# Expert capacities in unequal pairs, the sort of places behind the routing, and the last norm ahead of the overflow test

## The chip, the cores and the metric

The kernel runs on one core of a Trainium2 chip. The metric is the device time of one execution in microseconds (us). TensorE (PE) multiplies and loads its weights (PEld), VectorE (DVE), ScalarE (ACT) and GpSimd (POOL) do the rest, and SyncE (SP) issues nearly all of the large transfers. All data is fp32.

## The reference, cut to what matters

Two transformer blocks follow each other on 256 tokens of width 1024. The second one ends in a mixture of experts, and the change lies there:

```python
def moe_ffn(h, ...):                       # h: 256 tokens x 1024
    logits = h @ w_router + b_router       # 32 experts
    top_val, top_idx = lax.top_k(logits, 4)
    gate_w = softmax(top_val)
    # each token goes to its 4 experts e:
    hb = x[e] @ w_exp_in[e] + b_exp_in[e]  # 1024 -> 2 x 1024
    g, u = min(hb[:1024], 7), clip(hb[1024:], -7, 7)
    a = g * sigmoid(1.702 * g) * (u + 1)
    y = a @ w_exp_out[e] + b_exp_out[e]    # 1024 -> 1024
    # out: sum over the 4 experts of gate_w * y
h = layer_norm(DEEPNORM_ALPHA * h + moe_ffn(h), ln2_g, ln2_b)
```

The weights of one expert are 12 MB in fp32, those of all 32 are 403 MB, and every expert has tokens.

## The kernel before, in words

The first third (37 weight loads of 2 MB, the attention and retention block, the first feed-forward part, the second attention) is untouched. Then comes the router: `chosen` (line 859) takes the top 4 of each token tile, two matmuls with a triangular matrix (lines 913 and 915) number the tokens of each expert, and `pg` (line 917) holds each token's place in its expert.

**Places and capacities.** The 32 experts are worked on in an order of places 0 to 31. Place r has room for `caps(r)` tokens (line 125): 128, 64 or 32. Places 0 and 1 are always experts 0 and 1 (`FIXED`). The other places are given out at run time by `sort_experts` (line 947): the experts are ranked by their number of tokens, and the fullest one gets the place with most room (`_places`, line 1350). The table `SLOTS` (line 27) gives one capacity for each pair of places, so that both places of a pair have the same one; in order: 64, 32, 32, 128, 32, 32, 128, 32, 32, six times 64, 32. If an expert has more tokens than its place holds, `overflow` (line 1199) does the rest; a register load and an `If` on `most` decide that (lines 1151 and 1152).

**One expert.** `gather` (line 1019) runs once for a pair of places, during the odd place before it: it builds one-hot matrices (`one_hots`) and multiplies them with the normed tokens `hn`, 16 matmuls with as many columns as the pair has places for tokens. `hidden` (line 1051) runs 8 matmuls per quarter f of the first layer; since a place with 32 (64) tokens fills only a quarter (half) of the array's columns, 4 (2) of the eight run side by side. `gated` brings the result back into columns (transposes, or the `fold` matmuls where c is 32) and applies the activation, `out_rows` multiplies with the second layer, `weigh` applies the gate on ACT and DVE, and `scatter` (8 matmuls) adds the result to the four accumulators `acc`.

**Weights.** `Stream` (line 43) loads the weights through SP in program order, 2 MB for each transfer (line 69), six for an expert: four for the first layer, two for the second. In the expert stage the ring has nine such slots (three `w`, three `wh`, and `ring2`, `ring3`, `more4`), so a load waits until PE has read what lay in its slot nine loads before. From place 2 on, SP has to know the expert's number: 30 register loads of `ids` (line 152, `part`), placed in SP's queue among the weight loads. `ids` is made in the middle of `sort_experts` (line 977).

**When the sort runs.** `sort_experts` is a generator whose pieces run at the steps named in `SORT` (line 31): the first one, up to the sorted `posm` and `gtok`, is started at place 0 after its third quarter. Its tiles are the accumulators (`scr`), its table `places` is loaded by GpSimd at that point (line 959).

**Second norm.** `normed` (line 849) scales and shifts `hn`. For the first token tile it runs on DVE; for the second one, columns 0 to 511 go to ACT (line 853) and GpSimd (line 854), the others to DVE.

**The end.** After the last `scatter` comes the test for overflow, and after the `If` the last layer norm (lines 1156 to 1196), which writes the output in four transfers.

Within TensorE's queue and the others the order is set by a scheduler at build time, from the program order and estimated durations.

Of the kernel before, what the change touches and what calls it, by code (L numbers as in the profile page):

```python
# [26 lines left out]
SLOTS = (64, 32, 32, 128, 32, 32, 128, 32, 32, 64, 64, 64, 64, 64, 64, 32)  # L27
# [3 lines left out]
SORT = ((0, 2), (0, 3), (3, 1), (18, 1), (20, 1))  # L31
# [93 lines left out]
def caps(r):  # L125

    return SLOTS[r // 2]


def build(nc, tc, ctx, a, dbg=None):  # L130
# [662 lines left out]
    aid = mo.tile([128, 128], F32, name="aid")  # L793
    V.tensor_scalar(aid, ident, ALPHA, None, op0=OP.mult)
# [73 lines left out]
    def one_hots(r0, pos):  # L868

        c = caps(r0)  # L870
        oh = mo.tile([128, 2, 2, 128 // c, c], F32, name="oneh")
        for t in range(2):
            for i in range(2):
                last = V.tensor_scalar(oh[:, t, i], iota[:, None, 1:c + 1].to_broadcast([128, 128 // c, c]),
                                       pos[:, t, r0 + i:r0 + i + 1], None, op0=OP.is_equal)
        return oh, last
# [3 lines left out]
    for t in range(2):  # L880
# [25 lines left out]
        if t == 0:  # L906
            normed(t)
# [39 lines left out]
    def sort_experts():  # L947

        sp = mo
        b = scr[0][:, 0:2 * E].rearrange("p (i e) -> p i e", i=2)  # L950
# [7 lines left out]
        places = ep.tile([128, 128], F32, name="places", bufs=1)  # L958
        nc.gpsimd.dma_start(places, a["places"])
        bw = ep.tile([128, 512], F32, name="xs", bufs=3)  # L960
# [6 lines left out]
        b = scr[1][:, 0:2]  # L967
# [6 lines left out]
        b = scr[2][0:E, 0:2 * E].rearrange("p (i e) -> p i e", i=2)  # L974
# [6 lines left out]
        b = scr[3][:, 0:128]  # L981
# [3 lines left out]
        b = scr[0][:, 0:4 * E].rearrange("p (j t e) -> p j t e", j=2, t=2)  # L985
# [11 lines left out]
        yield  # L997

        bw = ep.tile([128, D], F32, name="xs", bufs=3)
        for t in range(2):  # L1000
            nc.gpsimd.dma_start(bw[64 + t * E:64 + (t + 1) * E, :], a["bout"])
        for n in range(2):
# [16 lines left out]
    def gather(r0):  # L1019
# [3 lines left out]
        c = caps(r0)  # L1023
        oh, _ = first if r0 == 0 else one_hots(r0, posm)
        xs = [ep.tile([128, 8, c], F32, name="xs", bufs=3) for _ in range(2)]
        for i in range(2):
            slots_of[r0 + i] = [xs[i]]
        per = min(8, 256 // c)
        for at, k0 in enumerate(range(0, 8, per)):
            b = (em.tile([128, 512], F32, name="m") if r0 else scr[at])[:, 0:per * 2 * c]  # L1030
            b = b.rearrange("p (k i c) -> p k i c", k=per, i=2)
            for kk in range(per):
# [3 lines left out]
            for i in range(2):  # L1036
                (A.copy if i else V.tensor_copy)(xs[i][:, k0:k0 + per], b[:, :, i, :])
            yield
        for i in range(2):
            b = em.tile([128, 2], F32, name="m")  # L1040
            for t in range(2):
                T.matmul(b, oh[:, t, i].rearrange("p d c -> p (d c)"), gtok[:, t, r0 + i, :],
                         start=t == 0, stop=t == 1)
# [105 lines left out]


# [4 lines left out]

    e1 = pool(ctx, "e1", 1)
    rows = ws.next()
# [269 lines left out]
```

## Time and profile before

| what | value |
|---|---|
| time, median of 3 runs | 1485.1 us (1479.3 to 1487.65) |
| time of the profiled execution | 1477.87 us |
| its span, first to last instruction | 1476.1 us |
| granted TensorE clock, mean | 0.978 of full speed |
| PE busy | 1394.0 us (94%) |
| DVE, ACT, POOL busy | 657.4, 433.6, 36.7 us |
| moved by DMA | 495.15 MB, 335 GB/s over the span |

The page divides the span into 40 slices of 36.9 us. A digit is the busy share in tenths, and the last line the rate of all transfers. The expert stage is in slices 14 to 39. PE reads as busy nearly throughout, also where a matmul only waits in its pipeline, so its busy share says little; the rate of the transfers says more.

### The profile page before, as it was taken

What the parts mean: (1) busy time and instruction counts of PE and PEld (TensorE: products, weight loads), DVE (VectorE), ACT (ScalarE), POOL (GpSimd) and SP (SyncE); (2) the same over time, 40 slices, a digit from 0 to 9 for tenths busy, and PEclk for the clock granted to TensorE, in tenths of its full rate; (3) what the DMA queues carried; (4) which work ended last, traced back from release to release, by engine and by line L of the source; (5) the groups of instructions that cost most, each with busy time, mean ns of one, the idle gap of its engine ahead of it and who ended that gap; (6) DMA issues with size and microseconds to landing.
All of it is one profiled execution on the core that took longest, in us unless ns stands there. A gap on an engine that the chain in (4) does not pass through costs nothing. (4 is left out here: it accounts for less than half of the span.)

```text
span 1476.1 us, 21068 instructions
## 1 busy us (share of the span) xinstructions
PE 1394.0 (94%) x8401; PEld 882.1 (60%) x8402; DVE 657.4 (45%) x1622; ACT 433.6 (29%) x819; POOL 36.7 (2%) x54
## 2 busy tenths in 40 slices
PE   7998999989999899999999899998999999999984
PEld 7988999979999744544545444454343443443431
DVE  5868977866667533222123221232332333233313
ACT  4535655544565212121112211122111111111111
POOL 1001000010001100000000000000000000000000
PEclk9999999999999999899999999999999999999987
DMA  8435545535435989999989999899999999999995
GB/s 350 172 129 184 215 172 199 203 137 200 179 142 197 392 328 365 427 427 426 427 349 418 426 427 426 349 417 427 426 426 428 426 427 426 427 426 427 426 427 213
DMA packets 38008, 495.15 MB, mean 335 GB/s; under 512 B 4561, under 2 KB 4881, under 8 KB 8593
## 3 DMA queue, kind: packets, MB, share of 16 engines
q1 hardware_dynamic: 35424, 486.69, 79.8%
q0 software_dynamic: 2192, 6.88, 1.4%
q8 instruction: 68, 1.11, 0.3%
q14 instruction: 36, 0.29, 0.1%
q10 hardware_dynamic: 288, 0.18, 0.0%
HBM read 492.68 MB, written 1.05 MB: 334 GB/s over the span
## 5 line engine op out<-in xcount | busy, mean ns | idle before, releaser
L1060 PE MATMUL m<-w,xs 128*64 128x512 f32 (+2 forms) x1392 | 315.2, 611 | 10.3 <-DMA w<-in_wexp_dram 10.3
L1077 DVE TENSOR_TENSOR gu<-m,bexp 128x256 f32<-128x256 f32 (+2 forms) x128 | 51.1, 399 | 457.2 <-PE m L1074 310.9
L1060 PEld LDWEIGHTS m<-w,xs 128*64 128x64 f32 (+2 forms) x1392 | 102.3, 136 | 167.9 <-issue 157.3
L1063 ACT COPY hs<-m 128x512 f32<-128x512 f32 x128 | 74.9, 585 | 416.0 <-PE m L1060 416.0
L232 PE MATMUL b<-ah,wh 128*128 128x256 f32 x1552 | 194.3, 282 | 1.4 <-ACT wh L83 1.4
L232 PEld LDWEIGHTS b<-ah,wh 128*128 128x128 f32 x1552 | 187.6, 191 | 3.3 <-ACT wh L83 1.8
L105 DVE TENSOR_TENSOR wh<-w,wh 128x1024 fp32r<-128x1024 f32 (+1 forms) x152 | 174.2, 1180 | 31.7 <-ACT wh L104 31.7
L104 ACT ACTIVATE wh<-w 128x1024 fp32r<-128x1024 f32 (+1 forms) x154 | 148.7, 1019 | 79.8 <-PE b L232 43.4
L1097 PE MATMUL m<-w,ea 128*32 128x512 f32 (+2 forms) x672 | 141.6, 614 | 9.3 <-DMA w<-in_wexp_dram 6.3
L1060 PE MATMUL m<-wh,xs 128*32 128x512 f32 (+2 forms) x656 | 121.4, 597 | 8.4 <-DMA wh<-in_wexp_dram 8.1
L205 DVE SCALAR_TENSOR_TENSOR one<-m,gs,one 128x512 fp32r<-128x512 f32 x64 | 46.8, 749 | 129.1 <-ACT one L204 127.7
L1084 ACT ACTIVATE th<-gu 128x128 f32<-128x128 f32 (+2 forms) x128 | 38.4, 300 | 215.3 <-DVE gu L1082 215.3
L232 PE MATMUL b<-al,wh 128*128 128x256 f32 x776 | 99.4, 280 | 0.0
L232 PEld LDWEIGHTS b<-al,wh 128*128 128x128 f32 x776 | 94.5, 190 | 0.0
L1097 PE MATMUL m<-wh,ea 128*64 128x512 f32 (+2 forms) x352 | 85.5, 627 | 4.9 <-DMA wh<-in_wexp_dram 4.1
L1097 PEld LDWEIGHTS m<-w,ea 128*32 128x32 f32 (+2 forms) x672 | 40.6, 129 | 78.4 <-issue 55.9
L1112 PE MATMUL acc<-one,so 128*128 128x512 f32 x256 | 77.5, 423 | 9.7 <-ACT one L204 8.6
L1072 PEld LDWEIGHTS m<-fold,hs 128*128 128x128 f32 x448 | 56.6, 196 | 48.0 <-issue 35.9
L1060 PEld LDWEIGHTS m<-wh,xs 128*32 128x32 f32 (+2 forms) x656 | 35.5, 124 | 72.4 <-issue 66.0
L1112 PEld LDWEIGHTS acc<-one,so 128*128 128x128 f32 x256 | 43.0, 188 | 50.0 <-ACT one L204 29.0
L1035 PE MATMUL m<-oneh,hn 128*128 128x64 f32 (+2 forms) x480 | 69.0, 299 | 0.0
L204 ACT ACTIVATE one<-m,gs 128x512 fp32r<-128x512 f32 x64 | 42.5, 686 | 82.1 <-PE m L1097 82.0
(370 smaller groups left out, 1384.5 us busy)
## 6 DMA issues: line engine op xcount, KB each, us to landing
w<-in_wexp_dram SPq DMA_DIRECT2D x128, 2048.0 KB, 37.4
wh<-in_wexp_dram SPq DMA_DIRECT2D x63, 2048.0 KB, 37.5
w<-in_wpre_dram SPq DMA_DIRECT2D x37, 2048.0 KB, 7.9
w<-in_wpre_dram SPq DMA_DIRECT2D x4, 512.0 KB, 7.9
w<-in_wexp_dram SPq DMA_DIRECT2D x4, 512.0 KB, 30.3
tab<-in_tab_dram SPq DMA_DIRECT2D x1, 1152.0 KB, 10.0
xn<-in_x_dram SPq DMA_DIRECT2D x2, 512.0 KB, 5.0
ra<-in_rowv_dram POOLq DMA_DIRECT2D x2, 512.0 KB, 7.2
```

Source lines behind the costliest of these rows:

```text
L104: self.nc.scalar.activation(h[:, c], t[:, c], AF.Copy)
L105: self.nc.vector.tensor_tensor(l[:, c], t[:, c], h[:, c].bitcast(F32), op=OP.subtract)
L204: return (A.activation(hi, src, AF.Copy, scale=scale), V.scalar_tensor_tensor(lo, src, scale, hi.bitcast(F32), op0=OP.mult, op1=OP.subtract))
L205: V.scalar_tensor_tensor(lo, src, scale, hi.bitcast(F32), op0=OP.mult, op1=OP.subtract))
L232: T.matmul(p[:, m, :], x[:, k, c], y[:, k, :], start=i == m == k == 0, stop=i == 2 and k == nk - 1, skip_group_check=True)
L1035: T.matmul(b[:, kk], hn[:, t, f], oh[:, t, :, 0, :], start=t == 0, stop=t == 1)
L1060: T.matmul(b[g * c:(g + 1) * c], xs[:, k, :], w[:, kk, :], start=k < n, stop=k >= 8 - n, skip_group_check=True)
L1063: A.copy(h, b)
L1072: T.matmul(p[:, j, :], h[:, j * 128:(j + 1) * 128], fold, start=True, stop=True)
L1077: V.tensor_tensor(both, p[:, :, 0:c], bexp[:, r, f].rearrange("p j i -> p (j i)")[:, :, None].to_broadcast([128, 4, c]), op=OP.add)
L1097: T.matmul(ys[n][g * c:(g + 1) * c], ac[:, kk, :], w[:, kk, n * 512:(n + 1) * 512], start=(j == kk == 0) if c == 128 else j < 64 // c, sto ...
L1112: T.matmul(acc[t][n], so[:, t * 128:(t + 1) * 128], y[:, n, :], start=first and y is yh, stop=last and y is yl, skip_group_check=True)
```

## The change

1. `SLOTS` now has one capacity for each place, and a pair may have two different ones. The three capacities occur as often as before (4 times 128, 14 times 64, 14 times 32); the places with 128 are now 6, 10, 14 and 18, each followed by one with 32, where they were 6, 7, 12 and 13.
2. `gather` writes one tile `xs` for both places of a pair, in two buffers by turns, and copies each group of matmuls with one instruction, on DVE and ACT by turns. The one-hot matrices of a pair lie side by side, and the 16 matmuls take as many columns as both places have together (96, 128 or 160; before 64, 128 or 256).
3. `sort_experts` is cut into more pieces, uses tiles of the pool `em` and not the accumulators, and its first three pieces run between the steps of the first `gather`, before place 0. `places` is loaded long before, into the tile of `aid`, and `aid` is made after the sort.
4. `normed` of the second token tile runs on DVE alone, one half before `pg` and one after the one-hot matrices of places 0 and 1.
5. The last layer norm and the output stand ahead of the register load and the `If`; a second copy of them stands inside the `If`, behind `overflow`.

```diff
-SLOTS = (64, 32, 32, 128, 32, 32, 128, 32, 32, 64, 64, 64, 64, 64, 64, 32)
+SLOTS = ((64, 64, 32, 64, 32, 64) + 3 * (128, 32, 64, 32) + (128, 32, 64, 64) + 5 * (64, 32))
-SORT = ((0, 2), (0, 3), (3, 1), (18, 1), (20, 1))
+SORT = ((0, 1), (0, 2), (2, 1), (2, 3), (18, 1), (20, 1))
 def caps(r):
-    return SLOTS[r // 2]
+    return SLOTS[r]
...
-    def normed(t, *ins):
-        for c in half:
-            if t and not c.start:
-                A.activation(hn[:, t, c], hn[:, t, c], AF.Copy, scale=lr[t])
-                G.tensor_tensor(hn[:, t, c], hn[:, t, c], ln[:, 1, c], op=OP.add)
-                continue
-            with after(*ins):
-                V.scalar_tensor_tensor(hn[:, t, c], hn[:, t, c], lr[t], ln[:, 1, c], op0=OP.mult, op1=OP.add)
+    def normed(t, c, *ins):
+        with after(*ins):
+            V.scalar_tensor_tensor(hn[:, t, c], hn[:, t, c], lr[t], ln[:, 1, c], op0=OP.mult, op1=OP.add)
...
-    normed(1, last)
+    normed(1, half[0], last)
     V.scalar_tensor_tensor(pg[:, 0], b, 1.0, sel, op0=OP.add, op1=OP.mult)
     first = one_hots(0, pg[:, 0])
     done = first[1]
+    normed(1, half[1], done)
...
-        places = ep.tile([128, 128], F32, name="places", bufs=1)
-        nc.gpsimd.dma_start(places, a["places"])
...
-        xs = [ep.tile([128, 8, c], F32, name="xs", bufs=3) for _ in range(2)]
-        per = min(8, 256 // c)
+        xs = ep.tile([128, 8, c], F32, name=f"xs{r0 // 2 % 2}", bufs=1)
+        per = min(8, 512 // c)
...
-                    T.matmul(b[:, kk], hn[:, t, f], oh[:, t, :, 0, :], start=t == 0, stop=t == 1)
-            for i in range(2):
-                (A.copy if i else V.tensor_copy)(xs[i][:, k0:k0 + per], b[:, :, i, :])
+                    T.matmul(b[:, kk], hn[:, t, f], oh[:, t].rearrange("p i c -> p (i c)")[:, 128 - c0:128 + c1],
+                             start=t == 0, stop=t == 1)
+            (A.copy if at % 2 else V.tensor_copy)(xs[:, k0:k0 + n], b)
...
     todo = gather(0)
-    for _ in range(4):
-        next(todo, None)
     pend = None
     sort = sort_experts()
+    for _ in range(3):
+        next(sort)
+        next(todo, None)
...
     scatter(*pend, False, True)
     close(ex2)
+    rows = ws.next()
+    def last_norm(ctx):
...
+    with ExitStack() as so:
+        last_norm(so)
     n = nc.values_load(most[0:1, 0:1], min_val=0, max_val=S)
     with tc.If(n > 0):
         with ExitStack() as so:
             overflow(so, nc, tc, em, a, acc, hn, iota, ident, posm, gtok, bexp, ids, over)
-    e1 = pool(ctx, "e1", 1)
...
+        with ExitStack() as so:
+            last_norm(so)
```

In TensorE's queue, right behind the routing's two matmuls with `sel`, this stands before (`oneh,hn` is the gather, `gtok` the gate columns, `w,xs` the first layer of place 0, and `sel`, `ones`, `pg` belong to the sort):

```order
L913 MATMUL b<-sel,upper 128x64
L915 MATMUL b<-sel,ones 128x32
L1035 MATMUL acc_5287<-oneh,hn 128x128
L1035 MATMUL acc_5288<-oneh,hn 128x128
L1035 MATMUL acc_5287<-oneh,hn 128x128 x7
L1035 MATMUL acc_5288<-oneh,hn 128x128 x7
L1042 MATMUL m<-gtok,oneh 128x2 x4
L1060 MATMUL m<-w_4910,xs 64x512 x4
L1060 MATMUL m<-w,xs 64x512 x4
L953 MATMUL acc_5287<-ones,sel 32x32 x2
```

and this now:

```order
L910 MATMUL b<-sel,upper 128x64
L912 MATMUL b<-sel,ones 128x32
L951 MATMUL m<-ones,sel 32x32 x2
L951 MATMUL m<-sel,ones 32x32 x2
L1037 MATMUL acc_5286<-oneh,hn 128x128
L1037 MATMUL acc_5287<-oneh,hn 128x128 x8
L1037 MATMUL acc_5286<-oneh,hn 128x128 x7
L965 MATMUL m<-ones,key 128x2
L973 MATMUL m<-perm,key 32x32
L974 MATMUL m<-perm,cn 32x32
L1044 MATMUL m<-gtok,oneh 128x2 x4
L1061 MATMUL m<-w_4910,xs_5309 64x512 x8
```

The counting matmuls, the ranks and the sorted numbers now stand ahead of the first layer of place 0.

In SP's queue, around the ring's ninth load (`w`) and the next ones, this stands before:

```order
L69 DMA wh_5340<-in_wexp_dram 128x4096
L69 DMA w<-in_wexp_dram 128x4096
L69 DMA w_5361<-in_wexp_dram 128x4096
L69 DMA w<-in_wexp_dram 128x4096
L69 DMA w_5449<-in_wexp_dram 128x4096
L152 TENSOR_LOAD ids
L152 ISA x2
L69 ISA
L69 DMA w_5502<-in_wexp_dram 128x4096
```

and this now:

```order
L69 DMA wh_5363<-in_wexp_dram 128x4096
L69 DMA w<-in_wexp_dram 128x4096
L152 TENSOR_LOAD ids
L152 ISA x2
...
L69 DMA w_5384<-in_wexp_dram 128x4096
```

The register loads began behind the twelfth load of the expert stage; now the first of them stand right behind the ninth, 7, 6, 8 and 9 of them ahead of the next four loads.

At the end of DVE's queue this stands before (`one` is the last expert's weighing):

```order
L205 SCALAR_TENSOR_TENSOR one<-m,gs,one 128x512 x2
L1151 TENSOR_LOAD most
L1152 COMPARE_AND_BRANCH
...
L1152 UNCONDITIONAL_BRANCH
L1172 BN_STATS st<-acc_5287 128x6
L1172 BN_STATS st<-acc_5288 128x6
L1173 BN_AGGR mv<-st 128x2
```

and this now:

```order
L205 SCALAR_TENSOR_TENSOR one<-m,gs,one 128x512 x2
L1170 BN_STATS st<-acc_5286 128x6
L1170 BN_STATS st<-acc_5287 128x6
L1171 BN_AGGR mv<-st 128x2
...
L1193 TENSOR_TENSOR z<-z,w_10767 128x512
L1199 TENSOR_LOAD most
L1200 COMPARE_AND_BRANCH
```

The register load and the branch stood ahead of the norm and now stand behind its last instruction.

## Rows read from the trace of the kernel before

**Rows 1.** The page, rate of all transfers in 40 slices of the span.

```profile
GB/s 350 172 129 184 215 172 199 203 137 200 179 142 197 392 328 365 427 427 426 427 349 418 426 427 426 349 417 427 426 426 428 426 427 426 427 426 427 426 427 213
```

**Rows 2.** Windows: PE, PEld, DVE, ACT, POOL busy (instructions), clock, DMA share, GB/s.

```profile
760.00:780.00 20.00, 20.00 (x98) 8.69 (x96) 4.60 (x13) 3.80 (x7) 0.00 (x0) 1.00 0.70 267
940.00:960.00 20.00, 20.00 (x86) 8.37 (x87) 5.65 (x13) 3.76 (x7) 0.00 (x0) 1.00 0.71 275
555.00:560.00 5.00, 5.00 (x31) 3.27 (x28) 3.29 (x8) 2.27 (x4) 0.00 (x0) 1.00 0.47 118
610.00:615.00 5.00, 5.00 (x27) 4.16 (x30) 0.42 (x1) 0.37 (x1) 0.00 (x0) 0.50 1.03 439
```

**Rows 3.** Waits of SP's queue, whole span: total us, times, longest us.

```profile
SPq L69 <- PE m L1060: 225.1, 62, 14.7
```

**Rows 4.** Timeline of PE, a place with 128: start, us, line, op, tiles, count.

```profile
698.55 7.03 PE L1060 MATMUL m<-w,xs 128*128 128x512 f32 x16
705.42 0.60 PE L1074 MATMUL m<-ident,hs 128*128 128x128 f32 x4
705.86 7.03 PE L1097 MATMUL m<-wh,ea 128*128 128x512 f32 x16
```

**Rows 5.** Timeline of PE, a place with 32.

```profile
797.83 1.92 PE L1060 MATMUL m<-w,xs 128*32 128x512 f32 x16
799.69 1.08 PE L1072 MATMUL m<-fold,hs 128*128 128x32 f32 x8
800.60 1.03 PE L1042 MATMUL m<-gtok,oneh 128*128 128x2 f32 x8
...
809.99 2.44 PE L1112 MATMUL acc<-one,so 128*128 128x512 f32 x8 [0.77 <-ACT one L204]
```

**Rows 6.** Timeline of PE, a place with 64.

```profile
1117.42 3.65 PE L1060 MATMUL m<-wh,xs 128*64 128x512 f32 x16
1121.01 0.66 PE L1074 MATMUL m<-ident,hs 128*128 128x128 f32 x4
```

**Rows 7.** Timeline of PE, gathers with 64, 256 and 128 columns.

```profile
736.08 3.68 PE L1035 MATMUL m<-oneh,hn 128*128 128x64 f32 x32
...
839.16 1.97 PE L1035 MATMUL m<-oneh,hn 128*128 128x256 f32 x8
...
1149.36 1.95 PE L1035 MATMUL m<-oneh,hn 128*128 128x128 f32 x16
```

**Rows 8.** Timeline of DVE and POOL in the router.

```profile
510.81 0.29 DVE L864 TENSOR_TENSOR oneh<-iota,i 128x128 f32<-128x128 f32 x1
512.00 1.25 POOL L854 TENSOR_TENSOR hn<-hn,one 128x512 f32<-128x512 f32 x1 [0.29 <-ACT hn L853]
512.34 1.07 DVE L864 TENSOR_TENSOR oneh<-iota,i 128x128 f32<-128x128 f32 x1
```

**Rows 9.** Timeline of PE, first gather and a piece of the sort.

```profile
515.85 6.33 PE L1035 MATMUL acc<-oneh,hn 128*128 128x128 f32 x32 [0.93 <-DVE oneh L874]
...
526.48 0.31 PE L953 MATMUL acc<-ones,sel 128*32 128x32 f32 x4
```

**Rows 10.** Line 152 on SP: register loads, ns min/median/max, first and last start.

```profile
L152 SPq TENSOR_LOAD <-ids x30: 262/263/473, 541.6 to 561.9; - x30
```

**Rows 11.** Timeline of PE, the last matmul of place 0.

```profile
555.68 0.59 PE L1097 MATMUL m<-wh,ea 128*64 128x512 f32 x1
```

**Rows 12.** Timeline of PE and DVE at the end.

```profile
1457.98 2.23 PE L1112 MATMUL acc<-one,so 128*128 128x512 f32 x8 [0.77 <-ACT one L204]
...
1464.52 1.30 DVE L1172 BATCH_NORM_STATS2 st<-acc 128x6 f32<-128x512 f32 x2 [5.15 <-PEq L1152]
...
1472.00 0.69 DVE L1195 TENSOR_TENSOR z<-z,w 128x512 f32<-128x512 f32 x1
```

**Rows 13.** Line 1152 on PE's sequencer, the branch: ns min/median/max.

```profile
L1152 PEldq COMPARE_BRANCH  x1: 3670/3670/3670, 1460.7 to 1460.7; - x1
```

**Rows 14.** Timeline of PE, a gather with 64 columns at half clock.

```profile
606.86 7.09 PE L1035 MATMUL m<-oneh,hn 128*128 128x64 f32 x32
```

More of the change, by code (lines that the diff above doesn't have):

```diff
@@ L792, in build @@
         V.tensor_scalar(gtok[:, t, :, 1], gtok[:, t, :, 1], tok[:, t:t + 1], None, op0=OP.add)
-    aid = mo.tile([128, 128], F32, name="aid")
-    V.tensor_scalar(aid, ident, ALPHA, None, op0=OP.mult)
+    places = mo.tile([128, 128], F32, name="aid")
+    nc.gpsimd.dma_start(places, a["places"])
     ring3 = pool(ctx, "ring3")
@@ L906, in build @@
         if t == 0:
-            normed(t)
+            for c in half:
+                normed(t, c)
     chosen(0)
@@ L1041, in gather @@
             for t in range(2):
-                T.matmul(b, oh[:, t, i].rearrange("p d c -> p (d c)"), gtok[:, t, r0 + i, :],
-                         start=t == 0, stop=t == 1)
+                T.matmul(b, oh[:, t, i], gtok[:, t, r0 + i, :], start=t == 0, stop=t == 1)
             gs = ep.tile([128, 2], F32, name="gs", bufs=5)
@@ L1148, in build, with out @@
     close(ex2)
+    rows = ws.next()
+    def last_norm(ctx):
+        e1 = pool(ctx, "e1", 1)
+        z = e1.tile([128, 2, D], F32, name="z")
+        stat = e1.tile([128, 8], F32, name="stat")
+        st = e1.tile([128, 2, 6], F32, name="st")
+        mv = e1.tile([128, 2], F32, name="mv")
+        rr = e1.tile([128, 2], F32, name="rr")
+        def out(t, n):
+            nc.sync.dma_start(a["out"][t * 128:(t + 1) * 128, half[n]], z[:, t, half[n]])
+        with tc.manual_schedule(engines={ACT, DVE, mybir.EngineType.Pool}):
+            junk = [z[:, 1, half[n]] for n in range(2)]
+            for n in range(2):
+                A.activation(junk[n], acc[1][n], AF.Identity, accum_out=stat[:, n:n + 1])
+                V.bn_stats(st[:, n, :], acc[0][n])
+            V.bn_aggr(mv, st.rearrange("p n s -> p (n s)"))
+            V.tensor_scalar(stat[:, 4:5], mv[:, 1:2], 1e-5, None, op0=OP.add)
+            G.tensor_tensor(rr[:, 0:1], stat[:, 4:5], mhalf[:, 0:1], op=OP.pow)
+            V.tensor_scalar(stat[:, 5:6], stat[:, 0:1], stat[:, 1:2], -1.0 / D, op0=OP.add, op1=OP.mult)
+            for n in range(2):
+                A.activation(junk[n], acc[1][n], AF.Square, bias=stat[:, 5:6], accum_out=stat[:, 2 + n:3 + n])
+            for n in range(2):
+                V.scalar_tensor_tensor(z[:, 0, half[n]], acc[0][n], mv[:, 0:1], rows[:, half[n]], op0=OP.subtract, op1=OP.mult)
+            for n in range(2):
+                V.scalar_tensor_tensor(z[:, 0, half[n]], z[:, 0, half[n]], rr[:, 0:1], rows[:, D + n * 512:D + (n + 1) * 512],
+                                       op0=OP.mult, op1=OP.add)
+                out(0, n)
+                if n == 0:
+                    V.tensor_scalar(stat[:, 6:7], stat[:, 2:3], stat[:, 3:4], 1.0 / D, op0=OP.add, op1=OP.mult)
+                    V.tensor_scalar(stat[:, 6:7], stat[:, 6:7], 1e-5, None, op0=OP.add)
+                    G.tensor_tensor(rr[:, 1:2], stat[:, 6:7], mhalf[:, 0:1], op=OP.pow)
+            V.tensor_tensor(stat[:, 7:8], stat[:, 5:6], rr[:, 1:2], op=OP.mult)
+            A.activation(z[:, 1, half[1]], acc[1][1], AF.Identity, scale=rr[:, 1:2], bias=stat[:, 7:8])
+            V.scalar_tensor_tensor(z[:, 1, half[0]], acc[1][0], stat[:, 5:6], rows[:, half[0]], op0=OP.add, op1=OP.mult)
+            V.scalar_tensor_tensor(z[:, 1, half[0]], z[:, 1, half[0]], rr[:, 1:2], rows[:, D:D + 512], op0=OP.mult, op1=OP.add)
+            out(1, 0)
+            V.tensor_tensor(z[:, 1, half[1]], z[:, 1, half[1]], rows[:, half[1]], op=OP.mult)
+            V.tensor_tensor(z[:, 1, half[1]], z[:, 1, half[1]], rows[:, D + 512:], op=OP.add)
+            out(1, 1)
```

78 lines of the change are left out of this document (24 added, 54 removed).

## The prediction, made before the changed kernel ran

> **What bounds the kernel now.** I read the rate of the transfers first [rows 1]. From slice 16 on it stands at 426 to 428 GB/s, the highest rate of the page, except in slices 20 and 25 (349 each). So the expert stage is paced by the weight loads: 2 MB (2.097 million bytes) at 427 GB/s are 4.91 us, six for an expert 29.5 us. The windows then show what happens in the two weak slices: 267 and 275 GB/s for 20 us [rows 2]. That is (427 - 267) / 427 x 20 = 7.5 us and (427 - 275) / 427 x 20 = 7.1 us without a transfer, 14.6 us together. SP's queue says who was waited for: PE's first layer held up loads 62 times, for 14.7 us at the longest [rows 3]. A load can't start until PE has read the slot it goes to. Both stalls lie at the end of the two pairs of places with 128.
>
> PE's own time for a place comes from starts of neighbouring rows. With 128: 16 records of the first layer take 705.42 - 698.55 = 6.87 us, the transposes 0.44 [rows 4]; a place has four of each, and two more such groups of 16 in the second layer: 6 x 6.87 + 4 x 0.44 = 43.0, with 2.1 for the scatter 45.1 us. With 32: 6 x 1.86 + 4 x 1.0 for the fold + 2.4 for the scatter + 0.8 that it waits for ACT = 18.3 us [rows 5]. With 64: 6 x 3.59 + 4 x 0.58 + 2.4 = 26.2 us [rows 6]. A gather adds 3.5, 3.8 or 7.7 us for 64, 128 or 256 columns [rows 7], and 0.95 for the gate columns [rows 5], once for two places.
>
> So a pair of 128 costs PE 2 x 45.1 + 4.5 = 94.7 us against 59.0 us of loads: loads gain 35.7 us on PE. Four places with 32 cost 4 x 18.3 + 4.5 + 8.7 = 86 us against 118, and empty the ring. As 7.5 us of the 35.7 ended as a stall, the ring gives way for about **28 us**. (Nine slots would be 44; those in use and a transfer's latency take the rest. I go by 28.)
>
> **The unequal pairs.** The same places cost the same, in another order, so I follow how far the loads are ahead. At 555 to 560 us the loads stall (118 GB/s) [rows 2], so the ring is full: 28. Place 1 leaves it there. Places 2 to 5 (32, 64, 32, 64, two gathers) take 18.3 + 26.2 + 4.6 + 18.3 + 26.2 + 5.8 = 99.4 us of PE against 118: 28 - 18.6 = 9. Here 96 columns are put between the rows for 64 and 128 (3.6), 160 between 128 and 256 (4.8). Place 6, with 128, brings it to 9 + 15.6 = 25, below 28. The next three (32, 64, 32) take 62.8 us and two gathers, 4.6 and 5.8: 73.2 against 88.5, back to 10. One such round of four is 45.1 + 73.2 = 118.3 us for PE and 118.0 for the loads. So place 18, the last with 128, ends near 26, and the rest (64, 32) gives PE slack. Both stalls go: -14.6 us. The margin is 2 to 3 us in some 380 us of PE work, under 1%, so I take back 1.6 for a small stall: **-13.0**, between -14.6 (none) and -9.6 (PE 2% slower: 7.6 us less the margin).
>
> The fewer, longer copies and the two buffers of `xs` I cost at nothing: a gather writes the buffer of the pair before the last, which is read by then, and PE's rows carry the result. If that cover were gone, a copy of this kind would show as a wait of PE before the next first layer.
>
> **GpSimd out of the router.** On DVE the same comparison took 0.29 us for the first token tile and 1.07 for the second, which ran while GpSimd added its half [rows 8]. With GpSimd gone the routing ends 0.78 us earlier. DVE's extra half (0.74) comes behind the one-hot matrices, where PE is in the first gather for 6.33 us [rows 9] and takes the other columns first, so it is hidden there.
>
> **The sort at once.** Ahead of the first layer of place 0 PE now has four counting matmuls (0.3 [rows 9]), the rank, two small ones (0.4 each by the same row), and waits once for DVE between them, about 1 us by the 0.93 it waited for the one-hot matrices [rows 9]: 2.1 - 0.8 = 1.3 us later. About 1 us of such matmuls leaves place 0 in return. The loads come free 0 to 1 us later; I take **+0.5**, with -0.8 and +2 as ends.
>
> The numbers of the experts then exist near 524 us, not 541.3. The 30 register loads took SP from 541.6 to 561.9 [rows 10], with weight loads between them; they now run from about 524, and seven of them (0.6 us each) stand ahead of the load that place 0 frees near 529. What is late next is PE: the load after the stall at 555 went out at 556.98, and PE's last matmul of place 0 began at 555.68 and took 0.59 [rows 11]. So the register loads held it by at most 0.7 us, and I cost their move at **nothing**. The two POOL transfers of the sort only move within cover.
>
> **The end.** The last scatter ends near 1460.2 and the norm starts at 1464.52 [rows 12], so the test costs 4.3 us there, 3.67 of them PE's branch [rows 13]. Now the norm starts at 1460.3. The test comes behind it, beside the last output transfer. From the last DVE instruction (1472.00 + 0.69) to the end of the span at 1476.1 are 3.4 us. In the new order the register load (0.5) and a branch up to 3.7 long follow the norm, and then the closing steps of 1 us: 5.2 instead of 3.4. So -4.3 + 1.8 = **-2.5**, with -4.3 (test wholly hidden) and 0 as ends. The Trainium skill, "Runtime: NRT & Kernel Launch", section "Instruction fetch mechanics", says that a taken branch to a target outside the window of prefetched instructions waits for a fetch. By that rule the moved branch keeps its price, as in my sum; a branch at the row of other engines' compares would give the whole 4.3.
>
> **Sum.** -13.0 + 0.5 - 2.5 = -15.0 us. The profiled execution took 1477.87 us, 1.8 of it outside its span; it would take 1462.9. It lies 7.2 us under the median of the runs, 1485.1, so for runs like those I forecast 1485.1 - 15.0 = **1470.1 us**.
>
> **Rivals.**
> *The loads run through.* No stall comes back, and the one at 555 us goes too, as it falls into the register loads: 309 / 427 x 5 = 3.6 us [rows 2]. With the test hidden: -14.6 - 3.6 - 4.3 = -22.5, 1463 us. For it: SP was still loading registers until 556.7. Against it: PE freed the slot only then [rows 11].
> *PE sets the pace.* The rounds of 118.3 against 118.0 us leave no room. Were PE 4% slower than my sums, as by one more wait of 0.77 in each place with 32 [rows 5], it would lose 15 us over 380, 12 beyond the margin: -14.6 + 12 + 0.5 - 2.5 = -4.6, 1481 us. Against it: nothing in rows 4 to 6 left a gap.
> *Half clock in a place with 128, slower than before.* Among the experts, the clock once stood at 0.50, that is 1.2 GHz, from 605 to 617 us, with PE reading as busy for 5.00 of 5 us [rows 2]; a gather took 7.09 instead of 3.68 us [rows 14]. It fell behind a stretch of places with 32. Now each place with 128 stands behind a lighter place, and has no slack. One whole place at 1.2 GHz costs 45 us more: -15 + 45 - 3 of margin = +27, 1512 us. It decides from some 25 us of lost work, which needs 50 us at half clock. Against it: both pairs of 128 came behind four places with 32 and ran at full clock, and the stretch lasted 12 us. The Trainium skill, "TensorE: Matmul & The Clock Gate", section "Part 1: The HAM clock gate", says that activity releases a throttle that is there by default. By that rule a place with 128 brings its own release; the rows of the pairs agree.
>
> **How the numbers follow.** A measurement of this kernel tells about 0.5% (7.4 us) from no change. Forecast 60%, with 1464 to 1477 as its own range from the ends of the terms and the spread of the runs; loads run through 13%; PE sets the pace 21%; half clock 4%; 2% for something else. The range 1458 to 1482 takes in the first two and most of the third. Faster by over 0.5%: 0.77 (nearly all of the first, the second, a third of the third); within 0.5%: 0.18; slower: 0.05.
>
> **What would show it right or wrong.** Right: no 20 us window between 700 and 1430 us under 410 GB/s, the transfers of weights done 11 to 15 us earlier, the norm's first DVE instruction within 0.5 us of the last scatter, `ids` read from about 524 us, and the second comparison in the router at 0.3 us. Wrong in the first term: a window under 400 GB/s at place 10, 14 or 18, which is PE setting the pace, or clock below 1 beside it, which is the gate. Wrong in the last: over 5.5 us from the last DVE instruction to the end of the span.

## The result, and the profile after

The changed kernel took 1463.7 us (median of 4 runs, 1457.8 to 1467.4), the kernel before 1482.4 in the same session. The ratio is 0.9867, with a 95% interval of 0.982 to 0.9914. Two later sessions gave 0.9881 (0.9858 to 0.9903) and 0.9874 (0.9848 to 0.99). It is faster by about 19 us; forecast were 15.0. The time lies just below the forecast's own range, 1464 to 1477 us. One run of the kernel with equal pairs below, 1578.6 us at a granted clock of 0.842, was slow and is left out of its figures.

Read first, as before, is the rate of transfers, from the page of the changed kernel:

```profile
PEclk9999999999999989999999999999999999999997
...
GB/s 351 175 100 176 219 209 174 175 179 204 183 127 137 391 308 373 422 427 427 427 427 425 427 426 427 426 428 426 426 427 427 427 426 427 426 428 426 426 427 223
```

The two weak slices of [rows 1] are gone: from slice 17 (counted from 0, as the prediction does) to the last but one none is under 425. The windows that held the stalls [rows 2] now read (columns as there):

```profile
760.00:780.00 20.00, 20.00 (x98) 7.04 (x96) 7.16 (x24) 3.58 (x8) 0.00 (x0) 1.00 1.01 428
...
940.00:960.00 20.00, 20.00 (x56) 9.38 (x55) 6.11 (x15) 2.92 (x6) 0.00 (x0) 1.00 1.01 428
```

The waits of SP's queue:

```profile
SPq L69 <- PE m L1061: 383.3, 89, 10.7
```

Against [rows 3] the longest wait fell from 14.7 to 10.7 us, but the total rose from 225 to 383. SP waiting for a slot costs nothing while enough loads are queued behind one another; only a window with a low rate is lost time. So a total of waits says nothing here; the rate does.

The span fell by only 10.4 us, from 1476.1 to 1465.7, less than the runs show. The reason lies ahead of the change: the profiled execution reached the first gather at 520.22 us, against 515.85 [rows 9], while the second token tile's sums, which no edit touches, were already 5.2 us later. In two later profiles of the changed kernel these sums began at 504.25 and 506.34 us, against 504.31 before, so the 5.2 us differ from run to run and aren't the change's. So I measure from one fixed place to another: **from the start of the first gather to the start of the last scatter**, and then to the end. Timeline of PE and DVE:

```profile
517.52 0.29 DVE L859 TENSOR_TENSOR oneh<-iota,i 128x128 f32<-128x128 f32 x1
```

```profile
520.22 6.57 PE L1037 MATMUL acc<-oneh,hn 128*128 128x128 f32 x32
...
529.17 8.78 PE L1061 MATMUL m<-w,xs 128*64 128x512 f32 x32
...
1449.56 2.24 PE L1113 MATMUL acc<-one,so 128*128 128x512 f32 x8 [0.77 <-ACT one L204]
```

```profile
1451.84 1.30 DVE L1170 BATCH_NORM_STATS2 st<-acc 128x6 f32<-128x512 f32 x2 [0.89 <-PE acc L1113]
...
1459.31 0.69 DVE L1193 TENSOR_TENSOR z<-z,w 128x512 f32<-128x512 f32 x1
```

Gather to last scatter was 1457.98 - 515.85 = 942.1 us [rows 9, 12] and is 1449.56 - 520.22 = 929.3. Scatter to end of span was 18.1 and is 16.1. The ids are read from 528.6 us on (line 152 on SP), against 541.6 [rows 10]; counted from the second tile's sums that is 19.1 us behind them, against 37.3:

```profile
L152 SPq TENSOR_LOAD <-ids x30: 262/264/473, 528.6 to 548.6; - x30
```

### The profile page after: what moved, and what is told of

The parts are those of the page before. It is cut to its first block, busy times and chain, and to the rows that moved or that the text cites. A ratio compares the mean times of both kernels' runs of the same rounds, so it can differ in the third digit from the quotient of the medians.

```text
span 1465.7 us, 21024 instructions
## 1 busy us (share of the span) xinstructions
PE 1392.5 (95%) x8401; PEld 881.4 (60%) x8402; DVE 659.2 (45%) x1614; ACT 429.4 (29%) x805; POOL 35.4 (2%) x53
## 5 line engine op out<-in xcount | busy, mean ns | idle before, releaser
L1061 PE MATMUL m<-w,xs 128*64 128x512 f32 (+2 forms) x1392 | 301.9, 606 | 8.0 <-DMA w<-in_wexp_dram 8.0
L232 PE MATMUL b<-ah,wh 128*128 128x256 f32 x1552 | 197.6, 285 | 1.4 <-ACT wh L83 1.4
L1061 PEld LDWEIGHTS m<-w,xs 128*64 128x64 f32 (+2 forms) x1392 | 96.5, 134 | 167.3 <-issue 161.6
L232 PEld LDWEIGHTS b<-ah,wh 128*128 128x128 f32 x1552 | 191.1, 194 | 3.3 <-ACT wh L83 1.8
L1098 PE MATMUL m<-w,ea 128*32 128x512 f32 (+2 forms) x672 | 138.2, 623 | 10.3 <-DMA w<-in_wexp_dram 8.4
L1061 PE MATMUL m<-wh,xs 128*32 128x512 f32 (+2 forms) x656 | 127.7, 597 | 3.2 <-DMA wh<-in_wexp_dram 3.2
L1098 PE MATMUL m<-wh,ea 128*64 128x512 f32 (+2 forms) x352 | 88.9, 627 | 2.9 <-DMA wh<-in_wexp_dram 2.5
L1061 PEld LDWEIGHTS m<-wh,xs 128*32 128x32 f32 (+2 forms) x656 | 39.1, 128 | 69.1 <-issue 66.6
L1037 PE MATMUL m<-oneh,hn 128*128 128x96 f32 (+2 forms) x480 | 64.4, 283 | 0.0
```

The costliest lines, as they stand in the source:

```text
L232: T.matmul(p[:, m, :], x[:, k, c], y[:, k, :], start=i == m == k == 0, stop=i == 2 and k == nk - 1, skip_group_check=True)
L1037: T.matmul(b[:, kk], hn[:, t, f], oh[:, t].rearrange("p i c -> p (i c)")[:, 128 - c0:128 + c1], start=t == 0, stop=t == 1)
L1061: T.matmul(b[g * c:(g + 1) * c], xs[:, k, :], w[:, kk, :], start=k < n, stop=k >= 8 - n, skip_group_check=True)
L1098: T.matmul(ys[n][g * c:(g + 1) * c], ac[:, kk, :], w[:, kk, n * 512:(n + 1) * 512], start=(j == kk == 0) if c == 128 else j < 64 // c, sto ...
```

## The experiments

Twelve runs were made. "Gather to scatter" is the length just described, from each profile.

| kernel | us | ratio to before (95%) | gather to scatter | first 32 matmuls of place 0 |
|---|---|---|---|---|
| before | 1482 to 1483 | 1 | 942.1 | 7.3 (two of 16) |
| changed, three profiles | 1463.7, 1463.8, 1462.8 | see above | 929.3, 929.2, 926.4 | 8.78, 8.78, 7.09 |
| equal pairs | 1479.3 | 0.998 (0.9967 to 0.9993) | 943.0 | 7.09 |
| pairs only | 1467.5 | 0.9902 (0.9882 to 0.9923) | 927.1 | 7.09 |
| tight order | 1468.8 | 0.9892 (0.9848 to 0.9935) | 932.7 | 8.46 |
| old tail | 1466.9 | 0.9893 (0.9875 to 0.9911) | 926.3 | 7.09 |
| late sort | 1461.8 | 0.9861 (0.9841 to 0.9882) | 927.3 | 7.09 |
| old router | 1464.6 | 0.9891 (0.9866 to 0.9915) | 927.2 | 7.09 |
| long added matmuls | 1467.4 | 0.9909 (0.9885 to 0.9932) | 927.0 | 7.09 |
| small added matmuls, twice | 1462.3, 1461.1 | 0.9867 (0.9847 to 0.9888), 0.9857 (0.9832 to 0.9882) | 925.0, 924.8 | 7.09 |
| small added, late sort, GpSimd last | 1463.7 | 0.987 (0.9849 to 0.9892) | 927.3 | 7.09 |

### Is it the order of the places?

The changed kernel with the old order:

```diff
-SLOTS = ((64, 64, 32, 64, 32, 64) + 3 * (128, 32, 64, 32) + (128, 32, 64, 64) + 5 * (64, 32))
+SLOTS = tuple(c for c in (64, 32, 32, 128, 32, 32, 128, 32, 32, 64, 64, 64, 64, 64, 64, 32) for _ in range(2))
```

> The changed kernel with the places in equal pairs again (64, 64, 32, 32, 32, 32, 128, 128, ...), everything else as changed: one copy target for a pair, the early sort, the router without GpSimd, the norm ahead of the test. My theory, that the order of the places alone took the stalls away: two stalls of 5 to 8 us come back behind places 7 and 13, 10 to 15 us in all, so 13 us more than the changed kernel's 1463.7, 1477 us. Rival, that the longer copies into one buffer took them away: no window under 410 GB/s between 700 and 1430 us, and 1464 us.

Its windows:

```profile
760.00:780.00 20.00, 20.00 (x100) 8.62 (x98) 4.90 (x15) 3.80 (x7) 0.00 (x0) 1.00 0.67 256
...
940.00:960.00 20.00, 20.00 (x76) 8.21 (x75) 4.25 (x11) 3.27 (x6) 0.00 (x0) 1.00 0.68 258
960.00:980.00 20.00, 20.00 (x149) 9.65 (x148) 7.13 (x26) 5.32 (x11) 0.00 (x0) 1.00 0.92 376
```

Both stalls are back: 8.0 + 7.9 + 2.4 = 18.3 us without a transfer, worked out as in the prediction, and the kernel is 16 us behind the changed one. The rival of the longer copies falls: they are in this kernel too. The stalls are larger than those of the kernel before, though. There the window behind the second stall, which the prediction left out, lost 0.6 us more, so 15.2 in all:

```profile
960.00:980.00 20.00, 20.00 (x150) 10.40 (x143) 6.43 (x27) 4.89 (x11) 0.00 (x0) 1.00 0.98 415
```

In windows of 5 us from 500 to 700 us (those under 415 GB/s counted) this kernel lost 11.7 us and the kernel before 14.1. By the account the loads then entered the heavy pairs 2.4 us further ahead and met a full ring sooner, so that what an earlier part saves is given back at the stall. No run tests this alone, but the profiles agree: where no stall follows, as in the changed kernel, an early loss shows at the end (15.1 us lost and 929.3 from gather to scatter in its first profile, 11.8 and 926.4 in its third).

The complement is the kernel before with nothing but the new order and its gather:

```diff
-    return SLOTS[r // 2]
+    return SLOTS[r]
...
-        xs = [ep.tile([128, 8, c], F32, name="xs", bufs=3) for _ in range(2)]
+        xs = ep.tile([128, 8, c], F32, name=f"xs{r0 // 2 % 2}", bufs=1)
```

> The kernel before with nothing but the unequal pairs (the order of the places, the gather into one buffer for a pair, the one-hot matrices for two sizes); sort, router and tail as before. My theory: both stalls go, -13 us from 1482.4, so 1469 us, and the ids are read at about 541 us as before. Rival, that the early sort is needed for it (ids late hold up the loads once the ring has no slack to give): a stall stays somewhere between 555 and 700 us, and the gain is under 8 us, 1475 us or more.

It took 1467.5 us, 15.2 under before. Gather to scatter is 927.1, 15.0 under before. The windows of the stalls:

```profile
760.00:780.00 20.00, 19.95 (x104) 7.31 (x104) 8.32 (x26) 3.79 (x8) 0.00 (x0) 1.00 1.01 429
...
940.00:960.00 20.00, 20.00 (x56) 9.18 (x55) 6.11 (x15) 2.43 (x5) 0.00 (x0) 1.00 1.00 424
```

The ids were read from 539.1 us, as late as before, so the early sort isn't needed for the gain. In every profile of the table but that of the long added matmuls, gather to scatter less the time lost in these windows (of 5 us up to 700 us, of 20 us from there) is 912 to 915 us: the lost transfers make up nearly all of the differences.

### Does the ring give way for 28 us?

Two neighbouring pairs are exchanged, so that the second 128 comes sooner behind the first; the work is the same.

```diff
-SLOTS = ((64, 64, 32, 64, 32, 64) + 3 * (128, 32, 64, 32) + ...
+SLOTS = ((64, 64, 32, 64, 32, 64) + 2 * (128, 32) + 2 * (64, 32) + (128, 32, 64, 32) + ...
```

> The changed kernel with two neighbouring pairs of places exchanged: 128, 32, 128, 32, 64, 32, 64, 32 at places 6 to 13 in place of 128, 32, 64, 32, 128, 32, 64, 32. The work is the same. By my account of the ring (28 us that it gives way, 25 used in the changed kernel) the second 128 comes when 18 us are used and takes 15.6: 5 us without a transfer at place 8, one window of 20 us near 320 GB/s, and 1469 us. Rival, a ring that gives way for 40 us or more (nine slots are 44): no stall, 1464 us. Rival, that PE sets the pace: stalls of 5 us or more in every round of four places, here as in the changed kernel.

The windows at place 8:

```profile
780.00:800.00 20.00, 20.00 (x62) 9.06 (x64) 6.11 (x15) 2.42 (x5) 0.00 (x0) 1.00 0.99 415
800.00:820.00 20.00, 20.00 (x144) 11.85 (x140) 5.26 (x20) 4.88 (x10) 0.00 (x0) 1.00 0.84 338
```

There are 0.6 + 4.2 = 4.8 us without a transfer, at the place that the account gave. No other window from 700 to 1420 us is under 415. Gather to scatter is 3.4 us longer than in the two profiles of the changed kernel that share its 8.5 to 8.8 us for the first 32 matmuls.

The size agrees partly by luck. The expectation said 5 us; its own numbers give 18 + 15.6 - 28 = 5.6, and with the gather of 160 columns that place 7 has in this order the 18 become 25 - 29.5 + 18.3 + 5.8 = 19.6, and the stall 7.2. On the other side the account has no half clock, and TensorE stood at half clock just ahead of this stall:

```profile
740.00:760.00 20.00, 18.88 (x121) 10.82 (x114) 6.40 (x28) 3.77 (x8) 0.00 (x0) 0.83 1.00 426
```

```profile
752.99 1.91 PE L1098 MATMUL m<-w,ea 128*32 128x512 f32 x8 [0.37 <-DVE ea L1089]
755.65 3.78 PE L1113 MATMUL acc<-one,so 128*128 128x512 f32 x8 [0.76 <-ACT one L204]
759.23 7.37 PE L1061 MATMUL m<-w,xs 128*128 128x512 f32 x16
```

In the changed kernel the first two take 1.07 and 2.45 us at this point. From the first one's start to place 8 are 6.2 us here and 4.2 there, and the first 16 records of place 8 take 7.21 in place of 6.87 [rows 4]. So I estimate that 2.3 of the 4.8 us come from the clock and 2.5 from the order.

What the run shows is the place: the stall comes where the account put it. A ring of 40 us would have shown nothing here (19.6 + 15.6 + 2.3 = 37.5), and PE as the pace would have shown a stall in every round. That the ring gives way for 28 us and no more isn't shown; by the numbers of this run it would be 31 to 33.

### The tail

The old tail was put back into the changed kernel: `last_norm` behind the `tc.If`, without the copy inside it.

```diff
-    with ExitStack() as so:
-        last_norm(so)
     n = nc.values_load(most[0:1, 0:1], min_val=0, max_val=S)
     with tc.If(n > 0):
...
-        with ExitStack() as so:
-            last_norm(so)
+    e1 = pool(ctx, "e1", 1)
...
```

> The changed kernel with the last norm behind the overflow test again. My theory: from the last scatter's start to the norm's first instruction 6.5 us again in place of 2.3, from the last DVE instruction's start to the end of the span 4.1 in place of 6.4, so 2.0 us more, 1465.7 us (below what the times can tell, so the trace decides). Rival, that the test only costs where it lies and is hidden in the changed kernel by the output transfer: 4.2 us more.

Its rows for the last scatter, the norm's start and the last operation:

```profile
1444.32 2.23 PE L1113 MATMUL acc<-one,so 128*128 128x512 f32 x8 [0.77 <-ACT one L204]
```

```profile
1450.52 1.29 DVE L1174 BATCH_NORM_STATS2 st<-acc 128x6 f32<-128x512 f32 x2 [4.81 <-PEq L1154]
...
1458.00 0.69 DVE L1197 TENSOR_TENSOR z<-z,w 128x512 f32<-128x512 f32 x1
```

Scatter to norm is 6.2 us again (2.3 in the changed kernel), and the last operation to the end 4.1 (6.4). Scatter to end is 17.8, against 16.1 to 16.3 in the three profiles of the changed kernel. So the move is worth 1.4 to 2.0 us. The times, 1466.9 against 1463.7, don't tell the expected 2.0 from the rival's 4.2; the trace does. The rest of the test stays on the path, and its rows in the changed kernel say where:

```profile
L1200 SPq EVENT_SEMAPHORE  x9: 17/17/17, 1463.4 to 1464.0; - x9
...
L1200 DVEq EVENT_SEMAPHORE  x2: 21/21/21, 1463.9 to 1464.0; - x2
L1200 PEldq COMPARE_BRANCH  x1: 3330/3330/3330, 1452.2 to 1452.2; - x1
...
L1200 SPq COMPARE_BRANCH  x1: 53/53/53, 1460.4 to 1460.4; - x1
L1200 DVEq COMPARE_BRANCH  x1: 76/76/76, 1460.5 to 1460.5; - x1
```

PE's 3.33 us now lie beside the norm. SP branches at 1460.4 and issues its next event at 1463.4; DVE does so at 1460.5 and 1463.9. An obvious rival is that SP waits for the last output transfer. But that one, issued at 1460.0, landed 2.1 us later, 1.3 us ahead of SP's event, and SP's wait at line 1200 has no transfer as its releaser, as the wait at the end of the kernel before has (the first two views are of the changed kernel, the last of the kernel before):

```profile
DMA to landing us min/median/max: 2.1/2.1/2.1
```

```profile
SPq L1200 <- SPq L1200: 3.0, 1, 3.0
```

```profile
SPq L1415 <- DMA out_dram<-z: 1.4, 1, 1.4
```

DVE had such a gap behind its branch in the kernel before too, from 1459.7 to 1462.6 us, well ahead of the outputs. By the rule named in the prediction (the Trainium skill, "Runtime: NRT & Kernel Launch", section "Instruction fetch mechanics") that would be the fetch of a far target on these queues too. The rows of PE, DVE and SP agree with it in that the time goes with the branch; no row names a fetch. ACT's row (branch at 1458.5, next event at 1459.0) shows no such wait.

### The sort and the router

The sort goes back into place 0:

```diff
-SORT = ((0, 1), (0, 2), (2, 1), (2, 3), (18, 1), (20, 1))
+SORT = ((0, 1), (0, 2), (0, 3), (0, 3), (0, 3), (2, 1), (2, 3), (18, 1), (20, 1))
...
-        next(sort)
         next(todo, None)
...
-            if (r, f) in SORT:
+            for _ in range(SORT.count((r, f))):
```

> The changed kernel with the sort of the places moved back into place 0 (the ids about 15 us later). My theory, that the early sort is worth next to nothing: the first layer of place 0 starts 1 to 1.5 us earlier against the routing result, the loads after 555 us are as before, and the time is within 2 us of the changed kernel's. Rival, that the early ids are part of the gain, as SP's register loads no longer hold up weight loads behind place 0: 3 to 4 us more without a transfer between 530 and 600 us, 1467 us. If the second fall of the clock comes from the sort's waits, it is absent here.

The ids were read from 541.5 us on, and nothing else moved by more than the runs differ: 1461.8 us, and 927.3 from gather to scatter, within the changed kernel's 926.4 to 929.3. The rival (3 to 4 us more lost between 530 and 600) falls.

The router's half for ScalarE and GpSimd comes back:

```diff
+    A.activation(hn[:, 1, half[1]], hn[:, 1, half[1]], AF.Copy, scale=lr[1])
+    G.tensor_tensor(hn[:, 1, half[1]], hn[:, 1, half[1]], ln[:, 1, half[1]], op=OP.add)
...
-    normed(1, half[1], done)
```

> The changed kernel with ScalarE and GpSimd doing their half of the second token tile's scale and shift again. My theory: the second comparison takes 1.0 to 1.4 us in place of 0.29, and the routing result comes 0.8 us later behind the second tile's sums, so 1464.5 us, which only the trace can tell. Rival, that the one-hot half that VectorE takes over delays the gather by as much (0.74 us): first layer at the same distance from the sums as in the changed kernel.

Its comparison beside GpSimd:

```profile
510.94 1.25 POOL L915 TENSOR_TENSOR hn<-hn,one 128x512 f32<-128x512 f32 x1 [0.28 <-ACT hn L914]
...
511.27 1.07 DVE L859 TENSOR_TENSOR oneh<-iota,i 128x128 f32<-128x128 f32 x1
```

It takes 1.07 us, as in [rows 8], against 0.29 in the changed kernel. From the second tile's sums to the gather are 11.5 us here and before, and 10.7 in the changed kernel: the gather starts 0.8 us sooner, too little for the times. The rival looked at the first layer of place 0, and by that sign it holds: 19.7 us from the sums here, and 19.7 and 19.5 in the first two profiles of the changed kernel (18.1 in the third, with less half clock, see below). So whether any of the 0.8 reaches the first layer is open. The Trainium skill, "SBUF — State Buffer", section "SBUF: two separate sides", says that VectorE with two inputs and GpSimd share a pair of ports as an exclusive lock; these rows agree: the 1.07 us end 0.15 us after GpSimd's.

### The clock at the start of the experts

In the changed kernel's first profile TensorE ran at half clock (1.2 GHz) twice. Windows from 515 to 535 us, columns as in [rows 2]:

```profile
515.00:520.00 5.00, 1.91 (x16) 1.67 (x16) 4.30 (x19) 0.00 (x0) 1.11 (x2) 0.57 1.01 421
520.00:525.00 5.00, 5.00 (x28) 4.94 (x26) 3.41 (x16) 0.69 (x2) 0.00 (x0) 0.50 0.53 164
525.00:530.00 5.00, 4.14 (x30) 3.33 (x30) 2.81 (x14) 0.10 (x1) 0.00 (x0) 0.84 0.89 364
530.00:535.00 5.00, 5.00 (x20) 1.61 (x18) 0.00 (x0) 0.43 (x1) 0.00 (x0) 0.72 0.02 7
```

The first fall, from 515.7 to 526.0 us, stands in the profile of the kernel before too, from 511 to 521 us. The second, from 529.4 to 532.8, came behind the sort's wait of 0.86 us, and the first 32 matmuls of place 0 took 8.78 us in place of 7.09. Two runs of the unaltered kernel asked whether that is the change:

> The changed kernel once more, unaltered, beside the three that follow. Its profile had TensorE at half clock from 515.1 to 526.0 us and a second time from 529.7 to 532.6 us, behind the sort's short waits; the same code in the profile of the version with the old tail had only the first, of 7 us. Theory, that the second is chance from run to run: this profile can show either, with 7.1 us for the first 32 matmuls of place 0 where it is absent and 8.8 where it is there. Time 1464.

> The changed kernel a third time, beside the next one. If the second fall of the clock is chance, it is there in some of its profiles and not in others: so far there in three of the five profiles with the early sort and no added matmuls (changed kernel twice, tight order), absent in two (equal pairs, old tail) and in the one with the old router. Time 1463.7.

The one showed the second fall (8.78), the other did not:

```profile
517.06 4.97 PE L1037 MATMUL acc<-oneh,hn 128*128 128x128 f32 x32
...
524.41 7.09 PE L1061 MATMUL m<-w,xs 128*64 128x512 f32 x32
```

With it gather to scatter takes 929.2 and 929.3 us, without it 926.4: 2.8 us. Not all of that is the second fall. The first lasted 10 us in these two and 7 in the third, and the gather took 6.57 and 6.42 us in place of 4.97; to the second belong the 8.78 in place of 7.09. The old router and the late sort had the long first fall alone, and take 927.2 and 927.3. By these, which have other edits too, the second fall costs about 2 us and the longer first one about 1. All three profiles with the second fall (with the tight order's) have the early sort, and four others with the early sort, without the matmuls added below, have no second fall; of the four profiles with a late sort none has it. That the early sort brings it on is not shown.

If the half clock comes of PE's idle time, matmuls that nothing reads should prevent it:

```diff
+    def keep_busy(p, name, n, ins):
+        d = p.tile([128, 512], F32, name=name)
+        for _ in range(n):
+            with after(ins):
+                T.matmul(d, ident, ln[:, 0, 0:512], start=True, stop=True)
...
+            if t and k == 3:
+                keep_busy(ps, "b", 2, mm)
+        if t:
+            keep_busy(ps, "b", 11, mm)
```

> The changed kernel with 16 matmuls of 512 columns added whose result nothing reads: 2 and 11 while TensorE waits for the routing, 3 while it waits for the sort's rank. Theory, that the half clock of this stretch is the work that TensorE lacks while it waits: the granted clock stays at 1.00, the first gather takes 3.8 us as its like did among the places, in place of 5.0 to 6.6, no second fall, and place 0 starts 1.5 to 3 us earlier against the routing result; the loads and the end follow by as much, 1461 us. Rival, that the added matmuls themselves are in the way (0.23 us each, 2.5 us before the routing's own): place 0 no earlier, 1464 us or more.

Three more of them stand behind the rank's matmul. The clock stayed at 1.00, but the added work was mis-sized: eleven matmuls (22 records) filled 9.69 us where 2.8 were free, and the gather began 17.5 us behind the second tile's sums in place of 10.7.

```profile
511.14 9.69 PE L879 MATMUL b<-one,ident 128*128 128x512 f32 x22
520.66 0.33 PE L920 MATMUL b<-sel,upper 128*128 128x64 f32 x2
...
522.02 3.84 PE L1048 MATMUL acc<-oneh,hn 128*128 128x128 f32 x32
```

With 128 columns in each:

> As the run before with added matmuls that nothing reads, but cut to the waits: columns of 128 in place of 512, 3 ahead of the second half of the routing matmuls, 11 while TensorE waits for the routing, 3 while it waits for the rank. In that run each 512-column one took 0.88 us as two records, so 11 of them filled 9.7 us where 2.8 were free; the clock stayed at 1.00 and the gather took 3.84 us. Theory: now 0.24 us each (the gather's rate), so the routing result is as early as in the changed kernel (9.9 us behind the second tile's sums), the gather takes 3.8 us, the second fall of the clock is gone, and place 0 starts 7 us behind the routing result in place of 8.2 to 9.8; time 1461 us. Rival: the clock falls all the same, as these matmuls are too light: gather 5 to 6.6 us, 1464 us.

```profile
510.24 2.70 PE L879 MATMUL b<-one,ident 128*128 128x128 f32 x22
513.78 0.41 PE L920 MATMUL b<-sel,upper 128*128 128x64 f32 x2 [0.84 <-PE b L879]
...
515.22 3.84 PE L1048 MATMUL acc<-oneh,hn 128*128 128x128 f32 x32
...
521.45 7.09 PE L1072 MATMUL m<-w,xs 128*64 128x512 f32 x32
```

No half clock, a gather of 3.84 us in place of 4.97 to 6.57, and place 0 6.2 us behind the gather's start, against 7.4 to 9.0. It was run again beside the changed kernel:

> The version with the small added matmuls (3, 11 and 3, columns of 128, read by nothing) again, in the same session as the changed kernel. From its trace the last scatter came 4.3 us sooner behind the routing result than in the changed kernel's traces. Theory: that is real time, 1460 to 1461 us, 2 to 4 us under the changed kernel. Rival: it is within what the runs differ by, no gap over 1 us between the medians.

The traces give 1.4 to 4.5 us (924.8 and 925.0 against 926.4 to 929.3); the times, 1461.1 against 1462.8, have intervals that overlap. It is the best version by the trace, but not one that the times tell from the changed kernel.

The last run joined the small matmuls with the late sort, and gave the norm's last two operations to GpSimd:

```diff
-            V.tensor_tensor(z[:, 1, half[1]], z[:, 1, half[1]], rows[:, half[1]], op=OP.mult)
-            V.tensor_tensor(z[:, 1, half[1]], z[:, 1, half[1]], rows[:, D + 512:], op=OP.add)
+            G.tensor_tensor(z[:, 1, half[1]], z[:, 1, half[1]], rows[:, half[1]], op=OP.mult)
+            G.tensor_tensor(z[:, 1, half[1]], z[:, 1, half[1]], rows[:, D + 512:], op=OP.add)
```

> The changed kernel with the sort back in place 0, the small matmuls that nothing reads (3 and 11), and the last two operations of the norm on GpSimd in place of VectorE. Theory: place 0 starts 5.5 us behind the routing result; and VectorE, whose part of the test took 3.3 us behind its last instruction, is done 1.4 us earlier, so the end of the span comes 1 us nearer to the last scatter (from the norm's first instruction 12.9 us in place of 13.9); together 1458 us. Rival for the end: GpSimd's two operations (1.25 us each by the router's row) put the last output transfer as far back as VectorE's test was, 13.9 us or more.

Both parts missed. The half clock came back (5.46 us for the gather), and PE had two idle times of 0.84 us that I had not filled. The version before has one of them and no half clock; that the two are the cause was not tested. At the end

```profile
1452.74 1.62 POOL L1201 TENSOR_TENSOR z<-z,w 128x512 f32<-128x512 f32 x1 [1.14 <-ACT z L1197]
1454.44 1.26 POOL L1202 TENSOR_TENSOR z<-z,w 128x512 f32<-128x512 f32 x1
```

are later than DVE would have been, and from the norm's start (1446.39) to the end of the span (1461.8) are 15.4 us in place of 13.9. DVE passed the test by 1456.8, but SP, which branched at 1456.1, issued its next event at 1459.5:

```profile
L1209 SPq EVENT_SEMAPHORE  x9: 17/17/17, 1459.5 to 1460.1; - x9
...
L1209 DVEq EVENT_SEMAPHORE  x2: 21/21/21, 1456.8 to 1456.9; - x2
```

So in this run SP, which issues the last transfer, holds the end, and not DVE. In the changed kernel both pass at 1464.0.

## Why the prediction was right, by its steps

**The unequal pairs: right, the term too small.** -13.0 was forecast, and -15.0 measured by the pairs alone (gather to scatter; -15.2 in the times). That is the lower end of the term's range, -14.6, and a little more. Two sizes were off. The stalls of before were 15.2 us and not 14.6: the prediction read 426 to 428 GB/s in all slices but 20 and 25, but slices 21 and 26 have 418 and 417 [rows 1]. And "I take back 1.6 for a small stall" was not needed: no window of the changed kernel between 700 and 1400 us is under 420. The margin is about used up, though. In the old router's profile, where TensorE stood at half clock for 7 us near 600 us, place 18 ends in a stall of 1.7 us (that the one causes the other was not tested):

```profile
1080.00:1100.00 20.00, 20.00 (x115) 10.29 (x114) 5.78 (x17) 4.06 (x8) 0.00 (x0) 1.00 0.95 390
```

That the order alone makes the stalls is shown by the equal pairs. That the ring gives way for 28 us is not: the tight order shows a limit below 40.

**GpSimd out of the router: right at the gather.** 0.78 forecast, 0.8 measured to the gather's start; what of it reaches the first layer is open.

**The sort at once: mechanism right, size open by chance.** The first layer was to start 1.3 us later against the sums; it did by 1.1 in the first profile (8.95 from the gather less 7.05 before, less the 0.8). In the third profile, with the shorter first fall of the clock, it starts 0.5 earlier. Not foreseen was how much half clock comes: the longer first fall and the second one make 2.8 us when they happen. With the router the early part was put at +0.5 (-0.8 to +2); against the pairs alone it is 929.3 - 927.1 - 0.8 = +1.4 with the fall and -1.5 without it, the latter below the term's lower end.

**The ids' move: right, nothing.** The stall behind place 0 stayed. It is 118 GB/s in one window of 5 us before [rows 2], or 3.6 us; now

```profile
550.00:555.00 5.00, 5.00 (x26) 1.76 (x24) 2.38 (x9) 0.62 (x2) 0.00 (x0) 1.00 0.90 339
...
560.00:565.00 5.00, 5.00 (x26) 2.55 (x24) 2.19 (x4) 1.96 (x3) 0.00 (x0) 1.00 0.71 229
```

or 1.0 + 2.3 us.

**The end: right in direction, the term too large.** -2.5 forecast, -1.4 to -2.0 measured. The 4.3 us ahead of the norm went as forecast (5.15 of waiting on DVE became 0.89), but 2.3 came back behind it and not 1.8. From the end of the last DVE instruction to the end of the span are 5.7 us (1465.7 - 1459.31 - 0.69), and 5.7 and 5.9 in the other two profiles. The prediction had 5.2, and by its own sign, over 5.5, this term is wrong. I had priced the moved test by PE's branch; but that one's 3.33 us run beside the norm, and it is SP and DVE that are late there, 3.0 and 3.4 us behind their branches.

**Sum.** In the profile with the second fall: -15.0 - 0.8 + 2.2 (929.3 - 927.1) - 2.0 = -15.6 us from the sums to the end, against -15.0 forecast. That these agree is luck in part: the pairs gave 2.0 more than forecast, the early part took 0.9 more and the end gave 0.5 less. Without the second fall the profile gives 2.8 more, 18.4. The times give 18.7 to 20.2, more than the forecast by a quarter and over. What lies between the profiles and the times is not accounted for: the kernel before has one profile, of a run 4.5 us under its median (1477.9 against 1482.4).

**The rivals.** The loads didn't run through: the stall at 555 stayed and the test wasn't hidden. Its time of 1463 is the measured one, but that is chance: the runs of before came out 2.7 us under those that I had started from, and its gain of 22.5 us is as far from 18.7 as the forecast's 15.0. PE doesn't set the pace: in the changed kernel every window from 700 us on is full. No place with 128 ran at half clock there (the tight order's place 8 did, at its start); the windows at 0.83, from 1260 us on, have PE busy for 16 to 18 of 20 us and transfers at 423 GB/s or more, so they cost nothing.

## What to carry to other kernels

Where a stream of loads sets the time and compute works in lumps, write the account of the ring: how far each lump sets the loads back, and how far they can be set back before they stop. The same work in another order can then be judged before it runs; here the account named the place of the stall in the tight order, and its size only roughly. What is saved ahead of a stall seems not to count: in the equal pairs it came back in the stall. And leave room in the account for a few microseconds of half clock.

## What the runs showed of the hardware that was not expected

The clock of TensorE can fall a second time soon after it has risen (up at 526.0, down at 529.4 us in the first profile), behind a few small matmuls and waits of under 1 us; the same program does so in some executions (8.78 us for the first 32 matmuls of place 0) and not in others (7.09). A matmul on 128x128 weights with 512 columns of fp32 came to 0.88 us as two records, and one with 128 columns to 0.25 (2.70 us for eleven), the first being the rate of the first layer at a place with 128 (6.87 us for 16 records [rows 4]). At a place with 64, where two matmuls run side by side, a record takes 0.22 (7.09 for 32), near the 0.23 that the expectation had put on a whole added one.
